# Group norm scales spread by way of memory, and softplus on 128 partitions by 192 columns

## The chip, the cores and the metric

The kernel runs on one core of one Trainium2 chip. The metric is the device time of one execution in microseconds; the figure for the kernel before is the median of three runs. One further execution was profiled, and every row of the trace below comes from it.

## What is computed

The reference is one inference step of a hybrid backbone: two layers over 128 context tokens and 256 latent tokens, with D_MODEL = 1024, all in float32. In each layer a modulated RMS norm is followed by one wide input projection, whose columns feed three mixers (a bidirectional state-space scan, pooling, a spatial gating unit) and three gates; then come an output projection, a residual, and a SwiGLU FFN. Two small pieces of it matter here, both in the scan mixer:

```python
dt = jax.nn.softplus(dt_raw.reshape(bsz, seq, 2, SSD_HEADS) + dt_bias)        # 64 values a token
...
y = y_f + flip(y_b) + xs * d_skip[:, None]
y = y.reshape(bsz, seq, SSD_INNER) * jax.nn.silu(z)
return grouped_rms_norm(y, g_norm, SSD_GROUPS), s_f, s_b                      # 4 groups of 512 channels
```

grouped_rms_norm multiplies each token's 512 channels of a group by 1/sqrt(mean square + eps) and by a gain for each channel.

## The kernel before

All 384 tokens are held at once, as three tiles of 128 (NT = 3, TOK = 384). Activations lie with channels on the partitions and tokens in the columns, so a projection is 8 blocks of 128x128 weights against 384 columns. Each float32 product is made of three float32r matmuls (mm3, L165 to L167): the weights and the activations are split into a rounded high part and a remainder, and high x high, high x low and low x high are summed. The 512 KB weight blocks come in one after another through six raw buffers (L98, on SP's queue); ACT makes the high part (whi, L115), VectorE the remainder (wlo, L116), into four buffers each, three blocks ahead of use (LEAD).

The stage ssd of a layer begins with dt_unit, which projects dt and computes softplus as max(x, 0) + log1p(exp(-|x|)), the logarithm by a polynomial. The weight block of dt holds its 64 columns twice, so the projection fills all 128 partitions of its PSUM tile with two equal halves; before, only the lower 64 are used, with all 384 tokens as columns. From dt follow the running sums (fs), which go out to memory (fsd) and come back spread over the partitions (fb). Then come, group by group (g = 0 to 3), a projection for B and one for C, and four pairs of heads, each with an X and a Z projection; between them stand filler projections whose results are spilled to memory.

The program counts these main units (tick) and posts later steps so many units behind them (post, with the lags L_...). gnorm1 (lag 7) sums the squares of a group over the partitions on TensorE, and VectorE makes the scale of each token from it: yr, 128 tokens by 3, tokens on the partitions. gnorm2 (lag 9) needs these scales along the columns, the same on all partitions. It makes them with three float32 matmuls of yr, broadcast, against the identity (L904), into a PSUM tile of tag tr (two buffers), which ACT copies to the SBUF tile ysq (L906, one buffer, also used for squares). Then VectorE scales the four tiles of the group (ynf, reading yg), and ACT and VectorE split them into yh and yl. sproj (from lag 14) multiplies them with the branch weights. For the last group gnorm1 and gnorm2 stand between fillers, without lags.

TensorE's instructions are issued in the order of the program (manual_schedule); the order on the other engines and on SP's queue, which issues all DMAs of these stages, is set by the planner of the framework from priorities and its own times. Each engine works through its queue in order.

Of the kernel before, what the change touches and what calls it, by code (L numbers as in the profile page):

```python
# [9 lines left out]
F32 = mybir.dt.float32  # L10
# [3 lines left out]
ACTF = mybir.ActivationFunctionType  # L14
ALU = mybir.AluOpType
# [5 lines left out]
NT = 3  # L21
TOK = 384
DEPTH = 2
# [23 lines left out]

FILL = ((3, 0, 2, 2, 1), (2, 1, 1, 2, 1), (1, 0, 1, 2, 1), (0, 0, 1, 1, 0))

L_TURN, L_TURN2, L_CB, L_DEC, L_XN, L_ST, L_Y, L_G1, L_G2, L_SP = 6, 7, 3, 3, 3, 5, 7, 7, 9, 14  # L50
T_G1, T_G2, T_G3 = 1, 1, 2
FIRST = (4,)
M1, M2 = (0, 1), (1, 2)
# [69 lines left out]
class Net:  # L123
# [67 lines left out]
    def build(self):  # L191
        tc, nc, ctx = self.tc, self.nc, self.ctx
        self.base = ctx.enter_context(tc.tile_pool(name="base", bufs=1))
        self.psum = ctx.enter_context(tc.tile_pool(name="psum", bufs=1, space=PSUM))
        self.psbufs = {"mm": 4, "tr": 2, "y": 1, "st": 1}
        dram = ctx.enter_context(tc.tile_pool(name="dram", bufs=1, space=DRAM))
        self.gd = dram.tile([DEPTH, 2, 2, D], F32, name="gd")
        self.xd = dram.tile([DEPTH, NT, 128, D], F32, name="xd")
        self.vd = dram.tile([DEPTH, NT, 128, D], F32, name="vd")
        self.ud = dram.tile([DEPTH, KT, 128, TOK], F32, name="ud")  # L200
        self.thd = dram.tile([DEPTH, 3, KT, 128, TOK], F32, name="thd")
        self.fsd = dram.tile([DEPTH, NH, 2, TOK], F32, name="fsd")
        b = self.base
        self.ident = b.tile([128, 128], F32, name="ident")
        self.mlo = b.tile([128, 128], F32, name="mlo")
        self.mup = b.tile([128, 128], F32, name="mup")
        self.smask = b.tile([64, TOK], F32, name="smask")
        self.edge = b.tile([128, 32], F32, name="edge")
        self.ones = b.tile([128, 1], F32, name="ones")
        self.selm = b.tile([128, 2], F32, name="selm")  # L210
        self.crow = b.tile([128, 2, D], F32, name="crow")

        self.hthl = b.tile([128, 2 * KT * TOK + 32], F32R, name="hthl")
        self.hthi, self.htlo = (self.hthl[:, HO + n * KT * TOK:HO + (n + 1) * KT * TOK].rearrange("p (k t) -> p k t", t=TOK) for n in range(2))
        self.accx = b.tile([128, NT * D], F32, name="accx")
        self.acc = self.accx.rearrange("p (c t) -> p c t", t=TOK)
        self.x = self.accx.rearrange("p (i d) -> p i d", d=D)
        self.flow = Flow(tc, nc, self.io["w"], b)
        self.cp, self.mod, self.xnorm, self.parts, self.vr, self.fnat = {}, {}, {}, {}, {}, {}
        self.pool = None  # L220
        self.flow.add([], self.start)
        for l in range(DEPTH):
            self.layer(l)
        self.flow.run()
        self.close_pool()
# [357 lines left out]
    def ssd(self, l):  # L583
        F = self.flow
        F.add([], lambda: self.ssd_open(l))
        self.main([("dt", l)], lambda w: self.dt_unit(l, w))
        fill = [("u", 0, c) for c in range(KT)] + [("g", br, c) for br in range(3) for c in range(KT)][:3 * KT - ORDER.count("g")]
        def filler(n):
            for _ in range(n):
                if fill:  # L590
                    kind, br, c = fill.pop(0)
                    if kind == "u":
                        self.main([("in", l, C_U + 128 * c)], lambda w, c=c: self.u_spill(l, c, w))
                    else:
                        self.main([("in", l, C_G + D * br + 128 * c)], lambda w, br=br, c=c: self.gate_spill(l, br, c, w))
        for g in range(4):
            self.main([("in", l, C_B + 128 * g)], lambda w, g=g: self.conv_unit(l, 16 + g, w))
            self.main([("in", l, C_C + 128 * g)], lambda w, g=g: self.conv_unit(l, 20 + g, w))
            if g == 0:
                self.post(L_TURN, lambda: self.turn(0))  # L600
                self.post(L_TURN2, lambda: self.turn(1))
            self.post(L_CB, lambda g=g: self.cb_unit(l, g))
            filler(FILL[g][0])
            for t in range(4 * g, 4 * g + 4):
                self.main([("in", l, C_X + 128 * t)], lambda w, t=t: self.conv_unit(l, t, w))
                self.post(L_DEC, lambda t=t: self.decay(l, t))
                self.post(L_XN, lambda t=t: self.xnat(l, t))
                self.post(L_ST, lambda t=t: self.states(l, t))
                self.post(L_Y, lambda t=t: self.ypair(l, t))
                if l == 0 and t < 2:  # L610
                    F.add([], lambda t=t: self.silu_row(t))
                self.take((t % 2 == 1) + (l == 0 and t % 4 == 2))
                self.main([("in", l, C_Z + 128 * t)], lambda w, t=t: self.z_unit(l, t, w))
                if t < 15:
                    filler(FILL[g][1 + t % 4])
            if g == 3:
                break
            self.post(L_G1, lambda g=g: self.gnorm1(l, g))
            self.post(L_G2, lambda g=g: self.gnorm2(l, g))
            for cc in range(4):  # L620
                self.post_main(L_SP + cc, [("brs", l, g, cc)], lambda w, g=g, cc=cc: self.sproj(l, g, cc, w))
        while self.late and len(fill) > T_G1 + T_G2 + T_G3:
            filler(1)
        self.flush_all()
        filler(len(fill) - T_G2 - T_G3)
        F.add([], lambda: self.gnorm1(l, 3))
        filler(len(fill) - T_G3)
        F.add([], lambda: self.gnorm2(l, 3))
        filler(len(fill))
        F.add([], lambda: [self.th_load(l, 0, c) for c in range(3)])  # L630
        for cc in range(4):
            self.main([("brs", l, 3, cc)], lambda w, cc=cc: self.sproj(l, 3, cc, w))
# [53 lines left out]
    def dt_unit(self, l, w):  # L686
# [1 line left out]
        cp = self.cp[l][0]  # L688
        ps = self.ps("mm")
        self.proj(ps, w)  # L690
        zz = self.t(pool, "arg", [128, TOK], 2)[0:64]
        self.act(zz, ps[0:64, 0:TOK], ACTF.Identity, bias=cp[0:64, CP_DTB:CP_DTB + 1])
        e = self.t(pool, "W", [128, 2 * TOK], 2)[0:64, 0:TOK]
        self.act(e, zz, ACTF.Abs)
        self.act(e, e, ACTF.Exp, scale=-1.0)
        mx = self.t(pool, "arg", [128, TOK], 2)[0:64]
        self.ts(mx, zz, 0.0, ALU.max)
        s = self.t(pool, "wb", [128, TOK], 2)[0:64]
        self.ts(s, e, 2.0, ALU.add)
        nc.vector.reciprocal(out=s, in_=s)  # L700
        self.tt(s, s, e, ALU.mult)
        s2 = self.t(pool, "W", [128, 2 * TOK], 2)[0:64, 0:TOK]
        self.tt(s2, s, s, ALU.mult)
        p = self.t(pool, "ysq", [128, TOK], 1)[0:64]
        self.ts(p, s2, 1.0 / 15, ALU.mult)
        for n in (13, 11, 9, 7, 5, 3):
            self.stt(p, p, 1.0 / n, s2, ALU.add, ALU.mult)
        self.stt(p, p, 1.0, s, ALU.add, ALU.mult)
        dtt = self.t(pool, "dtt", [64, TOK], 1)
        self.stt(dtt, p, 2.0, mx, ALU.mult, ALU.add)  # L710
        ea = self.t(pool, "ea", [64, 1], 1)
        self.act(ea, cp[0:64, CP_AL:CP_AL + 1], ACTF.Exp)
        la = self.t(pool, "ysq", [128, TOK], 1)[0:64]
# [177 lines left out]
    def gnorm1(self, l, g):  # L891
        nc, pool = self.nc, self.pool
        sp = self.ps("st")
        for c in range(NT):
            nc.tensor.matmul(sp[:, c:c + 1], lhsT=self.ysum[:, c * 128:(c + 1) * 128], rhs=self.ones, start=True, stop=True)
        ss = self.t(pool, "ss3", [128, NT], 2)
        nc.vector.tensor_copy(out=ss, in_=sp[:, 0:NT])
        self.yr = self.rstd_of(ss, 512, pool)

    def gnorm2(self, l, g):  # L900
        nc, pool = self.nc, self.pool
        rp = self.ps("tr")
        for c in range(NT):
            nc.tensor.matmul(rp[:, c * 128:(c + 1) * 128], lhsT=self.yr[:, c:c + 1].to_broadcast([128, 128]), rhs=self.ident, start=True, stop=True)  # L904
        rb = self.t(pool, "ysq", [128, TOK], 1)
        nc.scalar.copy(out=rb, in_=rp[:, 0:TOK])  # L906
        hls = []
        for t in range(4 * g, 4 * g + 4):
            yn = self.t(pool, "ynf", [128, TOK], 2)
            self.stt(yn, self.yg.pop(t), self.cp[l][0][:, CP_GS + t:CP_GS + t + 1], rb, ALU.mult, ALU.mult)  # L910
            hi = self.t(pool, "yh", [128, TOK], 4, F32R)
            lo = self.t(pool, "yl", [128, TOK], 4, F32R)
            self.split(hi, lo, yn)
            hls.append((hi, lo))
        self.yhl[g] = hls
# [454 lines left out]
```

## Time and profile before

| | before |
|---|---|
| median of 3 runs | 1843.42 us (1841.96 to 1846.58) |
| the profiled execution, time | 1843.37 us |
| the profiled execution, span in the trace | 1841.5 us |
| TensorE, matmul | 1809.9 us busy, 98% of the span, 10724 instructions |
| VectorE | 1448.9 us, 79% |
| ScalarE (ACT) | 969.0 us, 53% |
| weights (raw), from memory | 474 loads of 512 KB |

The profile's page gives busy time by engine, the span in 40 slices, the DMA queues, the chain of work that ended last, the costliest groups of instructions and the DMA issues. The trace behind it can be asked for the waits of an engine, for a timeline of single instructions in a stretch, and for busy times by stretch. A bracket at the end of a row says how long the engine was idle ahead of that instruction and what ended the idle time. Matmuls are pipelined and overlap in the rows, so their cost is read from start to start.

### The profile page before, as it was taken

Reading aid. Unit: us, or ns where it says so; the run is one execution under the profiler, and the core shown is the slowest. Engines: PE = TensorE matmul, PEld = TensorE weight load, DVE = VectorE, ACT = ScalarE, POOL = GpSimd, SP = SyncE. Lnnn points to the kernel's source line nnn. Section 1 sums busy time; section 2 is a strip of 40 time slices with the busy share of each in tenths; the row PEclk is TensorE's granted clock in tenths of the full one; section 3 lists DMA queues with packets and bytes.
Section 4 is the critical chain, followed back from the end, with each engine's and each line's share of the span. In section 5 each row is a group of like instructions: output and inputs, shape, how many; then the busy total and the mean of one; then the engine's idle time right before and its main releaser. Section 6 shows DMA issues by size and latency. Waiting matters only on the chain.

```text
span 1841.5 us, 28979 instructions
## 1 busy us (share of the span) xinstructions
PE 1809.9 (98%) x10724; PEld 1710.4 (93%) x10724; DVE 1448.9 (79%) x2891; ACT 969.0 (53%) x1916; POOL 0.2 (0%) x4
## 2 busy tenths in 40 slices
PE   7999999999999999999999999999999999999998
PEld 4899999999999889889879999999999997998997
DVE  4699989998979687877668989799977797644545
ACT  4687768584443453223355977685834434432332
POOL 0000000000000000000000000000000000000000
PEclk9999999999999999999999999999999999999999
DMA  8666564644757555765545655555455583554441
GB/s 334 236 232 221 187 191 159 212 133 141 265 197 251 171 174 182 247 191 183 191 166 181 223 178 196 158 166 195 133 164 208 189 274 127 170 160 126 126 126 46
DMA packets 112293, 341.15 MB, mean 185 GB/s; under 512 B 12948, under 2 KB 38420, under 8 KB 112024
## 3 DMA queue, kind: packets, MB, share of 16 engines
q1 hardware_dynamic: 112152, 339.30, 56.3%
q8 instruction: 84, 1.38, 0.3%
q14 instruction: 57, 0.47, 0.1%
HBM read 314.38 MB, written 24.87 MB: 184 GB/s over the span
## 4 chain that ended last, share of the span: by engine, by line
PE 91%; DVE 5%; DMA 2%; issue 1%; ACT 1%; SPq 0%; DVEq 0%; ACTq 0%
PE ps_mm L165 22%; PE ps_mm L167 22%; PE ps_mm L166 22%; PE ps_mm L460 5%; PE ps_mm L461 5%; PE ps_mm L462 5%; PE ps_y L879 3%; DMA raw<-w 1%; DVE wlo L116 1%; DVE ajunk L298 1%; PE ps_st L844 1%; PE ps_tr L826 1%; PE ps_mm L1080 1%; PE ps_mm L553 1%; PE ps_mm L555 0%
## 5 line engine op out<-in xcount | busy, mean ns | idle before, releaser
L115 ACT CAST whi<-raw 128x1024 fp32r<-128x1024 f32 x394 | 412.8, 1050 | 535.1 <-PE ps_mm L166 220.7
L165 PE MATMUL ps_mm<-hthl,whi 128*128 128x384 f32 x1936 | 656.6, 339 | 0.0
L167 PE MATMUL ps_mm<-hthl,wlo 128*128 128x384 f32 x1936 | 651.2, 336 | 2.6 <-DVE wlo L116 2.6
L166 PE MATMUL ps_mm<-hthl,whi 128*128 128x384 f32 x1936 | 649.9, 336 | 0.0
L116 DVE TENSOR_TENSOR wlo<-raw,whi 128x1024 fp32r<-128x1024 f32 x394 | 480.9, 1221 | 212.4 <-ACT whi L115 210.9
L167 PEld LDWEIGHTS ps_mm<-hthl,wlo 128*128 128x128 f32 x1936 | 363.8, 188 | 2.9 <-DVE wlo L116 2.9
L165 PEld LDWEIGHTS ps_mm<-hthl,whi 128*128 128x128 f32 x1936 | 364.1, 188 | 2.3 <-issue 1.5
L166 PEld LDWEIGHTS ps_mm<-hthl,whi 128*128 128x128 f32 x1936 | 364.0, 188 | 0.3
L298 DVE CUSTOM_DVE_ANT_0 ajunk<-raw,crow 128x1024 bf16<-128x1024 f32 x160 | 195.4, 1221 | 35.5 <-DMA raw<-w 34.0
L460 PE MATMUL ps_mm<-whi,ah 128*128 128x512 f32 (+1 forms) x360 | 141.4, 393 | 4.8 <-DVE res L147 4.5
L462 PE MATMUL ps_mm<-whi,al 128*128 128x512 f32 (+1 forms) x360 | 141.0, 392 | 0.0
L461 PE MATMUL ps_mm<-wlo,ah 128*128 128x512 f32 (+1 forms) x360 | 140.1, 389 | 0.0
L150 DVE SCALAR_TENSOR_TENSOR ca<-cin,cw,ca 128x388 f32<-128x388 f32 x192 | 118.2, 615 | 2.2 <-ACT ca L144 1.2
L165 PE MATMUL ps_mm<-ah,whi 128*128 128x384 f32 x288 | 98.2, 341 | 0.0
L166 PE MATMUL ps_mm<-al,whi 128*128 128x384 f32 x288 | 96.8, 336 | 0.3 <-DVE al L147 0.3
L167 PE MATMUL ps_mm<-ah,wlo 128*128 128x384 f32 x288 | 96.6, 336 | 0.0
L165 PE MATMUL ps_mm<-yh,whi 128*128 128x384 f32 x256 | 86.9, 339 | 0.0
L460 PEld LDWEIGHTS ps_mm<-whi,ah 128*128 128x128 f32 x360 | 68.3, 190 | 19.4 <-DVE res L147 4.9
L166 PE MATMUL ps_mm<-yl,whi 128*128 128x384 f32 x256 | 86.2, 337 | 0.0
L167 PE MATMUL ps_mm<-yh,wlo 128*128 128x384 f32 x256 | 86.1, 337 | 0.0
L461 PEld LDWEIGHTS ps_mm<-wlo,ah 128*128 128x128 f32 x360 | 68.2, 189 | 14.6
L462 PEld LDWEIGHTS ps_mm<-whi,al 128*128 128x128 f32 x360 | 68.1, 189 | 14.6
(234 smaller groups left out, 2417.1 us busy)
## 6 DMA issues: line engine op xcount, KB each, us to landing
raw<-w SPq DMA_DIRECT2D x474, 512.0 KB, 4.0
fb<-fsd SPq DMA_DIRECT2D x32, 768.0 KB, 4.2
thd<-spill SPq DMA_DIRECT2D x48, 192.0 KB, 4.9
spill<-thd SPq DMA_DIRECT2D x48, 192.0 KB, 4.1
araw<-wa SPq DMA_DIRECT2D x16, 512.0 KB, 8.5
s<-s SPq DMA_DIRECT2D x32, 128.0 KB, 2.1
so<-so SPq DMA_DIRECT2D x32, 128.0 KB, 3.1
k<-gd SPq DMA_DIRECT2D x8, 512.0 KB, 5.1
```

The costliest lines, as they stand in the source:

```text
L115: self.nc.scalar.copy(out=hi, in_=raw)
L116: self.nc.vector.tensor_tensor(out=lo, in0=raw, in1=hi.bitcast(F32), op=ALU.subtract)
L150: self.nc.vector.scalar_tensor_tensor(out=out, in0=a, scalar=s, in1=b, op0=op0, op1=op1)
L165: mm(out, lhsT=whi, rhs=xhi, start=first, stop=False)
L166: mm(out, lhsT=whi, rhs=xlo, start=False, stop=False)
L167: mm(out, lhsT=wlo, rhs=xhi, start=False, stop=last)
L298: self.nc.vector.tensor_tensor_reduce(out=junk, in0=raw, in1=self.crow[:, n, :], scale=0.5, scalar=0.0, op0=ALU.mult, op1=ALU.add, accum_o ...
L460: mm(out, lhsT=xh[:, ts], rhs=hi[:, ws], start=(kk == 0), stop=False)
L461: mm(out, lhsT=xh[:, ts], rhs=lo[:, ws], start=False, stop=False)
L462: mm(out, lhsT=xl[:, ts], rhs=hi[:, ws], start=False, stop=(kk == kn - 1))
L553: mm(av[i, q], lhsT=self.hthi[:, c, t], rhs=hi[:, ws], start=(c == 0), stop=False)
L879: mm(o, lhsT=lt, rhs=rt, start=(n == 0), stop=(n == steps - 1))
```

## The change

The scales of groups 0 to 2 of each layer no longer go over TensorE. gnorm1 ends with a store of yr to a new tensor in memory (grd), laid out so that the 384 tokens of a group stand in a row; a new step gnorm_row (lag 8) loads that row into all 128 partitions of a new tile rb; gnorm2 (now lag 10 instead of 9) uses rb. Group 3 keeps the matmuls, with rb in place of ysq. In dt_unit the lower 64 partitions take tokens 0 to 191 and the upper 64 tokens 192 to 383; softplus runs on 128 by 192, and two ACT copies put the halves side by side again.

```diff
-L_TURN, ..., L_Y, L_G1, L_G2, L_SP = 6, 7, 3, 3, 3, 5, 7, 7, 9, 14
+L_TURN, ..., L_Y, L_G1, L_GR, L_G2, L_SP = 6, 7, 3, 3, 3, 5, 7, 7, 8, 10, 14
...
+        self.grd = dram.tile([DEPTH, 4, NT, 128], F32, name="grd")
...
             self.post(L_G1, lambda g=g: self.gnorm1(l, g))
+            self.post(L_GR, lambda g=g: self.gnorm_row(l, g))
             self.post(L_G2, lambda g=g: self.gnorm2(l, g))
...
-        zz = self.t(pool, "arg", [128, TOK], 2)[0:64]
-        self.act(zz, ps[0:64, 0:TOK], ACTF.Identity, bias=cp[0:64, CP_DTB:CP_DTB + 1])
-        e = self.t(pool, "W", [128, 2 * TOK], 2)[0:64, 0:TOK]
+        HT = TOK // 2
+        zz = self.t(pool, "arg", [128, TOK], 2)[:, 0:HT]
+        for n in range(2):
+            r = slice(64 * n, 64 * n + 64)
+            self.act(zz[r], ps[r, n * HT:(n + 1) * HT], ACTF.Identity, bias=cp[r, CP_DTB:CP_DTB + 1])
+        e = self.t(pool, "W", [128, 2 * TOK], 2)[:, 0:HT]
...
-        mx = self.t(pool, "arg", [128, TOK], 2)[0:64]
+        mx = self.t(pool, "arg", [128, TOK], 2)[:, 0:HT]
...
-        s = self.t(pool, "wb", [128, TOK], 2)[0:64]
+        s = self.t(pool, "wb", [128, TOK], 2)[:, 0:HT]
...
-        s2 = self.t(pool, "W", [128, 2 * TOK], 2)[0:64, 0:TOK]
+        s2 = self.t(pool, "W", [128, 2 * TOK], 2)[:, 0:HT]
...
-        p = self.t(pool, "ysq", [128, TOK], 1)[0:64]
+        p = self.t(pool, "ysq", [128, TOK], 1)[:, 0:HT]
...
+        dth = self.t(pool, "wb", [128, TOK], 2)[:, 0:HT]
+        self.stt(dth, p, 2.0, mx, ALU.mult, ALU.add)
         dtt = self.t(pool, "dtt", [64, TOK], 1)
-        self.stt(dtt, p, 2.0, mx, ALU.mult, ALU.add)
+        for n in range(2):
+            nc.scalar.copy(out=dtt[:, n * HT:(n + 1) * HT], in_=dth[64 * n:64 * n + 64])
...
         self.yr = self.rstd_of(ss, 512, pool)
+        if g < 3:
+            nc.sync.dma_start(out=self.grd[l, g].rearrange("c p -> p c"), in_=self.yr)
+
+    def gnorm_row(self, l, g):
+
+        self.rb = self.t(self.pool, "rb", [128, TOK], 1)
+        self.nc.sync.dma_start(out=self.rb, in_=self.grd[l, g].rearrange("c p -> (c p)").partition_broadcast(128))
 
     def gnorm2(self, l, g):
         nc, pool = self.nc, self.pool
-        rp = self.ps("tr")
-        for c in range(NT):
-            nc.tensor.matmul(rp[:, c * 128:(c + 1) * 128], lhsT=self.yr[:, c:c + 1].to_broadcast([128, 128]), rhs=self.ident, start=True, stop=True)
-        rb = self.t(pool, "ysq", [128, TOK], 1)
-        nc.scalar.copy(out=rb, in_=rp[:, 0:TOK])
+        if g < 3:
+            rb = self.rb
+        else:
+            rp = self.ps("tr")
+            for c in range(NT):
+                nc.tensor.matmul(rp[:, c * 128:(c + 1) * 128], lhsT=self.yr[:, c:c + 1].to_broadcast([128, 128]), rhs=self.ident, start=True, stop=True)
+            rb = self.t(pool, "rb", [128, TOK], 1)
+            nc.scalar.copy(out=rb, in_=rp[:, 0:TOK])
```

## Rows read from the trace of the kernel before

**Rows 1.** The page, busy time by engine: us (share) x instructions.

```profile
span 1841.5 us, 28979 instructions
PE 1809.9 (98%) x10724; PEld 1710.4 (93%) x10724; DVE 1448.9 (79%) x2891; ACT 969.0 (53%) x1916; POOL 0.2 (0%) x4
```

**Rows 2.** The waits of TensorE: us in total, times, longest.

```profile
PE ps_mm L460 <- DVE res L147: 4.5, 1, 4.5
PE ps_mm L167 <- DVE wlo L116: 2.6, 1, 2.6
...
PE ps_tr L328 <- ACT ysq L906: 0.7, 1, 0.7
...
PE ps_tr L783 <- DVE ct L150: 0.2, 1, 0.2
```

**Rows 3.** Busy time by stretch, group 2 of layer 1: stretch, length, each engine.

```profile
1295.00:1330.00 35.00, 35.00 (x248) 33.97 (x247) 34.09 (x88) 31.75 (x83) 0.00 (x0) 1.00 0.44 139
```

**Rows 4.** Timeline of TensorE at gnorm2, group 0, layer 0: start, us, instruction.

```profile
199.98 0.33 PE L167 MATMUL ps_mm<-hthl,wlo 128*128 128x384 f32 x1
200.15 0.83 PE L904 MATMUL ps_tr<-ident,s3y 128*128 128x128 f32 x6
200.74 0.42 PE L165 MATMUL ps_mm<-hthl,whi 128*128 128x384 f32 x1
```

**Rows 5.** DMA issues: KB each, median us from issue to landing.

```profile
fb<-fsd SPq DMA_DIRECT2D x32, 768.0 KB, 4.2
thd<-spill SPq DMA_DIRECT2D x48, 192.0 KB, 4.9
...
fsd<-fs SPq DMA_DIRECT2D x4, 48.0 KB, 1.5
```

**Rows 6.** Timeline of SP's queue, group 2 of layer 1.

```profile
1304.27 0.33 SPq L798 DMA_DIRECT2D fb<-fsd  x1
1310.03 0.33 SPq L98 DMA_DIRECT2D raw<-w  x1
```

**Rows 7.** Timeline of VectorE, group 2 of layer 1.

```profile
1303.02 0.15 DVE L150 SCALAR_TENSOR_TENSOR s3y<-s3t,s3y 128x3 f32<-128x3 f32 x1
...
1307.68 1.15 DVE L150 SCALAR_TENSOR_TENSOR ynf<-yg,cp,ysq 128x384 f32<-128x384 f32 x2
...
1323.80 1.22 DVE L116 TENSOR_TENSOR wlo<-raw,whi 128x1024 fp32r<-128x1024 f32 x1
```

**Rows 8.** Timeline of TensorE, third matmul of the first sproj of that group.

```profile
1328.57 0.34 PE L167 MATMUL ps_mm<-yh,wlo 128*128 128x384 f32 x1
```

**Rows 9.** Timeline of VectorE, start of ssd in layer 1.

```profile
977.66 1.22 DVE L116 TENSOR_TENSOR wlo<-raw,whi 128x1024 fp32r<-128x1024 f32 x1 [1.14 <-ACT whi L115]
...
983.40 2.54 DVE L700 RECIPROCAL wb<-wb 64x384 f32<-64x384 f32 x1
...
990.59 0.27 DVE L150 SCALAR_TENSOR_TENSOR bt<-th,ca 128x128 f32<-128x128 f32 x1
990.79 0.54 DVE L150 SCALAR_TENSOR_TENSOR ysq<-ysq,W 64x384 f32<-64x384 f32 x1
991.26 0.41 DVE L150 SCALAR_TENSOR_TENSOR bt<-th,ca 128x256 f32<-128x256 f32 x1
991.59 0.54 DVE L150 SCALAR_TENSOR_TENSOR ysq<-ysq,W 64x384 f32<-64x384 f32 x1
...
995.07 1.21 DVE L116 TENSOR_TENSOR wlo<-raw,whi 128x1024 fp32r<-128x1024 f32 x1
...
999.57 1.20 DVE L116 TENSOR_TENSOR wlo<-raw,whi 128x1024 fp32r<-128x1024 f32 x1
```

**Rows 10.** Timeline of TensorE, same stretch: the waiting matmul, and that of the next block.

```profile
996.33 0.44 PE L167 MATMUL ps_mm<-hthl,wlo 128*128 128x384 f32 x1 [2.63 <-DVE wlo L116]
...
1001.59 0.34 PE L167 MATMUL ps_mm<-hthl,wlo 128*128 128x384 f32 x1
```

**Rows 11.** Timeline of ACT, same stretch.

```profile
1001.00 0.99 ACT L144 ACTIVATE wt<-fs,fe 64x128 f32<-64x128 f32 x3 [5.39 <-DVE fe L723]
```

More of the change, by code (lines that the diff above doesn't have):

```diff
@@ L48 @@
 FILL = ((3, 0, 2, 2, 1), (2, 1, 1, 2, 1), (1, 0, 1, 2, 1), (0, 0, 1, 1, 0))
-L_TURN, L_TURN2, L_CB, L_DEC, L_XN, L_ST, L_Y, L_G1, L_G2, L_SP = 6, 7, 3, 3, 3, 5, 7, 7, 9, 14
+L_TURN, L_TURN2, L_CB, L_DEC, L_XN, L_ST, L_Y, L_G1, L_GR, L_G2, L_SP = 6, 7, 3, 3, 3, 5, 7, 7, 8, 10, 14
 T_G1, T_G2, T_G3 = 1, 1, 2
```

## The prediction

> **What bounds the kernel now.** I read the page's table of engines first: TensorE is busy 1809.9 of the 1841.5 us span [rows 1]. It is the engine to follow, and its instructions are issued in the order of the program. So I then listed all that TensorE waited for [rows 2]. Behind the first 17 us, in which the inputs come in, the waits that bear on this case are few: 4.5 us for a residual product (L460 on res), 2.6 us for a weight split (L167 on wlo), 0.7 us for a PSUM slot (L328 on ysq), 0.2 us for the first B/C product (L783 on ct). Two more, for the norm ahead of the FFN, are untouched; all the rest is matmul after matmul. Two things can therefore shorten the run: an instruction taken out of TensorE's stream, or one of these waits. Work that is saved on another engine counts only through a wait. The third view, busy time by stretch, shows a second limit close by: around the group norm of group 2 in layer 1 VectorE is busy 34.09 of 35.00 us [rows 3]. What makes VectorE stand still there is not easily caught up.
>
> **Part 1, what leaves TensorE.** gnorm2 makes three float32 matmuls (L904), six records, that spread yr over the partitions. In the timeline L904 starts at 200.15, where the next L165 would have started (the matmul before began at 199.98, and they follow 0.17 apart), and L165 starts at 200.74 [rows 4]. That is 0.59 us of TensorE's time. Groups 0 to 2 of two layers lose them: 6 x 0.59 = 3.5 us. Group 3 keeps them. Nothing on TensorE takes their place.
>
> The copy L906 from PSUM goes with them, six times. It hides behind other ACT work nearly everywhere; the one place where TensorE waited for it is L328, 0.7 us, in group 1 of layer 0, where the transposition in ada_end wanted the PSUM slot that L906 was still reading [rows 2]. With one tr tile fewer the slot it gets was read long before. I count 0.7 us.
>
> **Part 2, what the row costs by way of memory.** Added are six stores of yr (384 separate numbers) and six broadcast loads of 192 KB, all on SP's queue; SP must hold the load until the store has landed. The trace has no store in such small pieces. Bounds: the smallest store with a landing time is fs to fsd, 1.5 us; the slowest small one is the spill, 4.9 us. The load is like fb from fsd, also a broadcast from memory, 4.2 us [rows 5]. With some 0.3 us for each issue [rows 6] the row is there 0.3 + 1.5 + 0.3 + 4.2 = 6.3 us to 0.3 + 4.9 + 0.3 + 4.2 = 9.7 us after yr, if SP is free. I take 6.3 to 7, since the store is nearest to that of fs (few bytes, from VectorE's result).
>
> The Trainium skill (DMA: Bandwidth & Descriptors, Rules for kernel authors) says that a transfer whose last dimension is not contiguous is cut into one descriptor per element, and should be rearranged; no run here shows such a store. By the same page's 10.5 ns a packet (Bandwidth) 384 pieces would take an estimated 4.0 us, inside the bounds above, and the sum stays.
>
> Who needs the row: only the four ynf products on VectorE, and behind them sproj. Before, in group 2 of layer 1, yr was done at 1303.2 and the first ynf began at 1307.7 [rows 7], 4.5 us later. gnorm2 is now posted one unit later (10 for 9); a unit is 24 matmuls of 0.17 us, 4.1 us at least. So ynf's turn comes some 8.6 us after yr, and the row is there in 6.3 to 9.7: hidden, or late by a us. And sproj, which uses what ynf makes, reaches its third matmul only at 1328.57, 20 us after the first ynf [rows 7, 8]. So I cost the detour at nothing (a gain is excluded: nobody gets the row sooner than before); its cover is the unit by which gnorm2 is put off. If the cover is gone, VectorE stands still and the weight splits behind ynf in its queue are late; that is priced as a rival. What SP queues behind the waiting load are raw weights, state loads and spills.
>
> rb also gets a buffer of its own and leaves ysq to the squares; TensorE waits for no square, so it counts nothing. The tiles that move up in the pool (ynf, yh, yl) are used again only late in the next stage.
>
> **Part 3, softplus.** Its 14 operations on VectorE up to dt halve in columns (192 for 384); the reciprocal is one of them. They stand at the start of ssd, once a layer. In layer 1 TensorE waits there 2.63 us, at 996.33, for the split wlo that VectorE began at 995.07, 17 us after the split before (977.66), just behind the chain's operations, with which those of the first two convolutions alternate without idle time [rows 9, 10]. So VectorE's time before 995.07 is on the path.
>
> What a narrower operation saves I take from starts, since VectorE overlaps ends: a 64x384 operation holds it 0.47 us (990.79 to 991.26), a 128x128 one 0.20 (990.59 to 990.79), a 128x256 one 0.33 (991.26 to 991.59) [rows 9]. So time goes by columns, and 192 columns come to about 0.265, a saving of 0.205. Between the reciprocal and 995.07 there are nine such (two products, seven fused ones): 1.85 us. The reciprocal takes 2.54 us for 384 columns [rows 9]; the trace has no other width, so its saving lies between 0 and 1.27; I take 1.27, as 6.6 ns a column is far above what an instruction's start can cost. The three tensor_scalars I leave at nothing. Sum 3.1 us: the split ends at 993.2 instead of 996.3, and TensorE wanted it at 996.33 - 2.63 = 993.70 [rows 9, 10]. The whole 2.6 us go, with half a us to spare; without the reciprocal's share 0.7 us of it would stay.
>
> What is late next is the split after it: it starts at 999.57, ends near 1000.8, and its matmul (1001.59) comes 2.6 us earlier, at 998.96 [rows 9, 10]. It gains the same 3.1 us plus 0.2 for the last product (dth), and loses what the detour of dt over ACT adds. That detour is two copies of 64x192; three 64x128 ones take 0.99 us [rows 11], so about 0.7 us. 1000.8 - 3.3 + 0.7 = 998.2, still in time. On ACT itself there are three operations more and two narrower ones, about 0.7 us a layer; ACT already waits 5.39 us in this very place for the chain's end [rows 11], so they hide in that. The copies' wait for dth queues spills and roundings behind it on ACT, for less than those 5.39 us. In layer 0 the same chain costs TensorE only the 0.2 us at L783 [rows 2], which goes too.
>
> **The sum.** 3.5 + 0.7 + 2.6 + 0.2 = 7.0 us. The profiled execution took 1843.37 us, of which 1841.5 is the span; its time stands at the median of the runs (1843.42), so no correction: 1843.4 - 7.0 = 1836.4 us. The wait at L460 [rows 2] and the two for the norm lie in the back part, which the change doesn't touch; they stay.
>
> **Rivals.** (a) Only the matmuls and L328 count; the wait of layer 1 stays or moves. The order on VectorE, ACT and SP is planned anew when operations change length, and a split may just be put behind other work; the margin is half a us. For it: in layer 1 a weight split stood 17 us behind the one before (977.66, then 995.07 [rows 9]), so the planner does let it slip. Against it: the sum of the work before it falls. 1843.4 - 4.2 = 1839.2 us.
>
> (b) The row comes late and VectorE stands still: the one that ends on the other side. Place: group 2, where the split that ends at 1324.9 is wanted at 1328.57, a margin of 3.6 us [rows 7, 8]; I take the same for layer 0, whose code is the same. Before, SP stood from 1304.6 to 1310.03 waiting for a raw buffer [rows 6]. If the store falls behind that, it is issued at 1310.4, lands 1.5 to 4.9 us later, and the row is there at 1316.4 to 1319.8, against ynf's turn at about 1311.8: VectorE stands 4.6 to 8 us. Beyond the margin TensorE loses 1 to 4.4 us, in both layers 2 to 8.8: 1838.4 to 1845.2 us, and 1845.2 is the rival's time. It passes the time before when the stand exceeds 7.1 us in both layers. The Trainium skill (DMA: Bandwidth & Descriptors, Rules for kernel authors) speaks for it: a DMA that reads what another wrote has to wait on the issuing engine for the first one's completion, so all that SP has behind it waits too; the trace of before has no such pair next to each other. Against it: the row is asked for two units ahead, so the planner has room to put the store first.
>
> (c) The change brings more: with other orders the 4.5 us of L460 [rows 2] go as well: 1836.4 - 4.5 = 1831.9 us. Nothing in the change is near it.
>
> (d) The change does not do what it says, for instance the planner puts ynf no later than before, so that the row is on the path from the start. Then all six groups wait a little, but only group 2 pays; this falls in (b).
>
> **How the numbers follow.** Chances: forecast 0.46, (a) 0.26, (b) 0.20, (c) 0.08. Predicted is the forecast, 1836.4. The range 1833.0 to 1843.5 leaves out (c) and the worst third of (b), about 0.15, and holds the ends for the reciprocal and the store. A measurement of this kernel tells some 0.3%, 5.5 us, from no change, so faster means under 1837.9. The forecast lies only 1.5 us below that: of its 0.46 I give 0.37 to faster and 0.09 to the same, of (a) 0.04 to faster, of (b) 0.01, all of (c): faster 0.50. Slower by over 5.5 us needs (b) at its worst and another wait: 0.06. The same: 0.44.
>
> **What would show it.** Right: six L904 groups gone and L165 following at 0.17; no wait at L328; the wait of L167 on wlo under half a us; 64x384 operations replaced by 128x192 ones that hold VectorE near 0.27 us and a reciprocal near 1.3; ynf begins without idle time of VectorE. Wrong: VectorE idle before ynf with a DMA of rb as its releaser, or SP held long between store and load; new waits of TensorE on wlo near 421 or 1328; a reciprocal much above 1.3 us; a wait that comes up in the back part.

## The result, and the profile after

The changed kernel takes 1876.01 us (1870.90 to 1879.35) against 1843.52 us of the kernel before in the same measurement: a ratio of 1.0171, interval 1.0157 to 1.0184. It is 32 us slower where 1836.4 us were forecast. The profiled execution took 1874.14 us; its span is 30.9 us longer than the 1841.5 us before [rows 1].

The page, busy time by engine:

```profile
span 1872.4 us, 28934 instructions
PE 1817.2 (97%) x10688; PEld 1713.5 (92%) x10688; DVE 1439.8 (77%) x2891; ACT 963.2 (51%) x1916; POOL 0.2 (0%) x4
```

TensorE has 36 records fewer (10688 for 10724: the six groups of six), VectorE and ACT are less busy, and yet the span grows. So look at waits, not at work. The waits of TensorE after (us in total, times, longest), to be held against [rows 2]:

```profile
PE ps_y L888 <- DVE se L147: 8.6, 4, 5.0
PE ps_y L888 <- DVE yg L150: 8.5, 3, 4.6
...
PE ps_tr L835 <- ACT bn L788: 2.3, 2, 2.0
PE ps_st L853 <- DVE ss L906: 2.2, 2, 1.3
PE ps_mm L167 <- DVE wlo L116: 2.1, 2, 1.4
...
PE ps_st L853 <- DVE xw L147: 1.8, 1, 1.8
```

None of these six stands in the list before, apart from wlo, whose wait there was another one (below). They lie in the groups, and come to 25.5 us. Two thirds are on ps_y, the product of a pair of heads (ypair, L888), which needs VectorE's se, or a PSUM slot that VectorE's yg must first have read. What VectorE and SP wait for there, first VectorE's list and then SP's:

```profile
DVE ynf L150 <- DMA rb<-grd: 47.4, 6, 8.9
```

```profile
SPq L914 <- DMA grd<-s3y: 49.4, 6, 9.5
```

VectorE stands before ynf in all six groups, 7.9 us each time on average, for the loaded row; and SP stands before the load, 8.2 us each, for the store to land. TensorE's stands of 3 us and more on ps_y lie in groups 0 and 2 of both layers; in groups 1 VectorE stands as long (5.94 and 8.19 us), but TensorE waits for it not at all in layer 0 and 1.6 us in layer 1. Group 0 of layer 0, in the timelines of SP, VectorE and TensorE:

```profile
199.93 0.38 SPq L909 DMA_DIRECT2D grd<-s3y  x1
201.06 0.34 SPq L98 DMA_DIRECT2D raw<-w  x1
209.44 0.33 SPq L914 DMA_DIRECT2D rb<-grd  x1
```

```profile
206.02 0.55 DVE L150 SCALAR_TENSOR_TENSOR sz<-th,ps_mm 128x384 f32<-128x384 f32 x1
215.42 1.15 DVE L150 SCALAR_TENSOR_TENSOR ynf<-yg,cp,rb 128x384 f32<-128x384 f32 x2 [8.85 <-DMA rb<-grd]
...
218.95 0.42 DVE L147 TENSOR_TENSOR se<-se,ps_st 128x256 f32<-128x256 f32 x1
```

```profile
214.01 0.39 PE L888 MATMUL ps_y<-cf,s 128*64 128x128 f32 x4
219.42 0.48 PE L888 MATMUL ps_y<-cf,se 128*64 128x128 f32 x2 [5.03 <-DVE se L147]
```

From store to load SP takes 9.5 us (209.44 - 199.93), from load to row 6 us. Over the six groups the first is 9.5, 9.5, 10.5, 10.0, 9.9 and 9.1 us. VectorE reaches ynf at 206.6 and stands 8.85 us. The pair of heads is due in the meantime; its se is only a 0.42 us sum, but it is queued behind ynf. TensorE stands 5.03 us.

Then a second loss begins. Busy time by stretch (stretch, length, engines, granted clock, DMA share, GB/s):

```profile
214.00:216.00 2.00, 0.39 (x8) 0.15 (x4) 0.58 (x2) 0.00 (x0) 0.00 (x0) 1.00 0.13 46
216.00:218.00 2.00, 0.00 (x0) 0.00 (x0) 2.00 (x6) 1.93 (x5) 0.00 (x0) 0.55 0.08 30
218.00:220.00 2.00, 0.58 (x6) 0.58 (x8) 2.00 (x5) 2.00 (x6) 0.00 (x0) 0.50 0.38 136
220.00:222.00 2.00, 2.00 (x16) 1.67 (x13) 2.00 (x8) 2.00 (x8) 0.00 (x0) 0.50 0.00 0
222.00:224.00 2.00, 2.00 (x11) 2.00 (x10) 2.00 (x4) 2.00 (x5) 0.00 (x0) 0.74 0.95 316
```

While TensorE stands, its granted clock falls to 0.50, the lower of its two levels (1.2 of 2.4 GHz), and stays there for some 3 us after the work goes on: in 220 to 222 it is fully busy at half speed. In the groups there are five such stretches (the first from 216.22, the last up to 1359.68). Taken together:

```profile
sum 23.85, PE 19.76 PEld 17.87 DVE 23.85 ACT 21.95 POOL 0.00; mean PE 3.95 PEld 3.57 DVE 4.77 ACT 4.39 POOL 0.00
```

Of the 23.85 us TensorE is busy for 19.76, so the lower clock costs it at most half of that, 9.9 us; in the other 4 us it stands anyway, and these are in the waits already. In the kernel before there is no such stretch in the groups.

The account: 25.5 us of waits, less the 0.7 at L328 that are gone, plus 9.9 of clock, less 4.0 of matmuls (six times 0.66, as measured below) and 2.8 of softplus waits, is 27.9; the spans differ by 30.9. The 3 us that are left are not worked out here.

### The profile page after: what moved, and what is told of

It is laid out like the page before. It is cut to its first block, busy times and chain, and to the rows that moved or that the text cites. A ratio compares the mean times of both kernels' runs of the same rounds, so it can differ in the third digit from the quotient of the medians.

```text
span 1872.4 us, 28934 instructions
## 1 busy us (share of the span) xinstructions
PE 1817.2 (97%) x10688; PEld 1713.5 (92%) x10688; DVE 1439.8 (77%) x2891; ACT 963.2 (51%) x1916; POOL 0.2 (0%) x4
## 4 chain that ended last, share of the span: by engine, by line
PE 80%; DVE 9%; DMA 7%; issue 2%; ACT 1%; SPq 0%; DVEq 0%; ACTq 0%
PE ps_mm L165 19%; PE ps_mm L166 19%; PE ps_mm L167 19%; PE ps_mm L462 5%; PE ps_mm L461 5%; PE ps_mm L463 5%; DMA grd<-s3y 3%; PE ps_y L888 2%; DVE wlo L116 2%; DMA raw<-w 2%; DMA rb<-grd 1%; DMA s<-s 1%; DVE ajunk L299 1%; DVE ca L150 1%; DVE wb L150 1%
## 5 line engine op out<-in xcount | busy, mean ns | idle before, releaser
L159 ACT CAST ah<-t 128x384 fp32r<-128x384 f32 x72 | 36.8, 512 | 92.7 <-DVE t L150 60.6
```

Of the source, the lines that this page charges most:

```text
L159: self.nc.scalar.copy(out=hi, in_=x)
```

## The experiments

Theory after the result: the 384 single numbers of the store land slowly; VectorE, which takes its queue in order, stands behind ynf for the row, and the operations behind it are what TensorE needs. Rivals: part of the loss is the softplus part's; SP, held between store and load, is the cause; any round trip through memory takes that long. Ratios are against the kernel before, run beside each kernel.

**Softplus alone** (the edits of gnorm1, gnorm_row and gnorm2 undone).

> Only the softplus part of the change; the scales go over TensorE as in the kernel before. Theory (the loss lies wholly in the row by way of memory, the softplus part brings what the trace of after shows): layer 1's wait of 2.6 us and the 0.2 us at L783 go, so about 1843.5 - 2.8 = 1840.7 us, ratio 0.9985. Rival (the two ACT copies and the wider partitions cost elsewhere, part of the 31 us is theirs): 1843.5 or above.

Measured: 1841.41 us, ratio 0.9983 (0.9974 to 0.9992), some 3 us faster than the 1844.26 beside it. TensorE's wait on wlo and the one at L783 are gone. This part does what the forecast said.

**The row alone** (the edits of dt_unit undone).

> Only the row by way of memory; softplus stays on 64 by 384. Theory: all of the loss is here: 1876.0 + 2.8 = about 1879 us (ratio 1.019), again with SP held 9 to 10.5 us between store and load and VectorE idle 8 to 9 us ahead of ynf. Rival (the two parts disturb each other, the order planned for one makes the other late): clearly below 1876.

Measured: 1881.27 us, ratio 1.0212 (1.0194 to 1.0229); VectorE's idle time before ynf is 51.8 us. All of the loss is here, 37 us where 36 were expected.

**The row loaded, but not read:**

```diff
-L_TURN, ..., L_GR, L_G2, L_SP = 6, 7, 3, 3, 3, 5, 7, 7, 8, 10, 14
+L_TURN, ..., L_GR, L_G2, L_SP = 6, 7, 3, 3, 3, 5, 7, 7, 8, 9, 14
...
-        if g < 3:
-            rb = self.rb
-        else:
-            rp = self.ps("tr")
...
+        rp = self.ps("tr")
...
+        rb = self.t(pool, "ysq", [128, TOK], 1)
+        nc.scalar.copy(out=rb, in_=rp[:, 0:TOK])
```

> As after, with the store and the load of the row in place, but nothing reads the loaded row: gnorm2 makes its scales with the matmuls of the kernel before, at the old lag. It separates the queue from the consumer. Theory (VectorE stands behind ynf for the row, and ypair and TensorE behind VectorE): without the reader the loss goes, about 1840 to 1843 us, although SP is still held 9 to 10 us between store and load. Rival (SP held is what costs: raw weights, state loads and spills behind the load come late): 1865 to 1876 us stays.

Measured: 1852.27 us, ratio 1.0043 (1.0028 to 1.0059). Between the two: without the reader some two thirds of the loss go, but 11 us against softplus alone stay. In the traces of the two kernels TensorE runs level (within 0.02 us) through both groups 0 and both groups 1; it loses 1.4 us in group 2 of layer 0 and 7.5 in group 2 of layer 1 (the other 2 us lie in the FFN). Group 2 of layer 1 on SP, on ACT and on TensorE:

```profile
1308.67 0.38 SPq L909 DMA_DIRECT2D grd<-s3y  x1
1309.73 0.32 SPq L807 DMA_DIRECT2D fb<-fsd  x1
1318.31 0.32 SPq L914 DMA_DIRECT2D rb<-grd  x1
...
1319.67 2.15 SPq L805 DMA_DIRECT2D s<-s  x1
```

```profile
1327.44 0.83 ACT L144 ACTIVATE se<-s,et 128x64 f32<-128x64 f32 x3 [7.52 <-DMA s<-s]
```

```profile
1333.98 0.77 PE L853 MATMUL ps_st<-xw,bn 128*128 128x256 f32 x1 [2.66 <-DVE xw L147]
```

The state load (L805) stands behind the held load of the row, is issued at 1319.67, and ACT waits 7.52 us for it; VectorE's chain of the next pair waits for ACT, and TensorE 2.66 us for xw, after which its clock is down again. So the store and the load cost something of their own, by what stands beside and behind them, but less, and mostly where VectorE has no slack: this is the group that was full before [rows 3]. Whether that is the hold of SP's queue this run doesn't tell: the state load, once issued, is itself used only 7.8 us later.

**The row from GpSimd's queue** (store and load issued there; SP is free).

> As after, but the store and the load of the row are issued from GpSimd's queue, which has nothing else to do; SP is never held by them. It takes the queue's share out of the 32 us. Theory (the reader on VectorE carries most; the held queue adds state loads and raw loads that come late, 8 to 11 us as where the row was loaded and not read): the row is as late as in after, VectorE idle 7 to 10 us before ynf, 1862 to 1870 us. Rival (the queue is the cause, VectorE's stand a side effect): 1845 us or below.

Measured: 1881.92 us, ratio 1.021 (1.0183 to 1.0236): no better, rather worse than after, and outside both expectations: the 8 to 11 us of the held queue did not come back. That SP is held is not the main cause. The DMA issues of this kernel (KB, median us to landing), and VectorE's list:

```profile
rb<-grd POOLq DMA_DIRECT2D x6, 192.0 KB, 5.5
grd<-s3y POOLq DMA_DIRECT2D x6, 1.5 KB, 9.8
```

```profile
DVE ynf L150 <- DMA rb<-grd: 56.7, 6, 10.8
```

The 1.5 KB store lands after 9.8 us from this queue too, and the row is still later. What is beside it is slowed as well. Stretches of this kernel behind the last store (issued at 1331.26; the load follows at 1341.63):

```profile
1334.00:1336.00 2.00, 2.00 (x24) 1.75 (x25) 2.00 (x6) 2.00 (x8) 0.00 (x0) 1.00 1.06 25
1336.00:1338.00 2.00, 2.00 (x23) 1.78 (x20) 0.58 (x1) 2.00 (x6) 0.00 (x0) 1.00 1.20 28
1338.00:1340.00 2.00, 2.00 (x13) 2.00 (x12) 0.00 (x0) 0.09 (x1) 0.00 (x0) 1.00 0.72 22
```

The last two columns are DMA share and GB/s. SP is not held here, and a load of 768 KB (fb) was issued at 1331.94, yet the DMA engines move 22 to 28 GB/s.

**Fewer, longer pieces.** Two kernels. In the first, each partition writes its three numbers as one piece of 12 bytes; in the second, yr is transposed first:

```diff
-            nc.sync.dma_start(out=self.grd[l, g].rearrange("c p -> p c"), in_=self.yr)
+            nc.sync.dma_start(out=self.grd[l, g].rearrange("c p -> (c p)").rearrange("(p c) -> p c", c=NT), in_=self.yr)
```

```diff
-            nc.sync.dma_start(out=self.grd[l, g].rearrange("c p -> p c"), in_=self.yr)
...
     def gnorm_row(self, l, g):
...
+        tp = self.ps("tr")
+        self.nc.tensor.transpose(out=tp[0:NT, 0:128], in_=self.yr, identity=self.ident)
+        row = self.t(self.pool, "rb", [128, TOK], 1)[0:NT, 0:128]
+        self.nc.scalar.copy(out=row, in_=tp[0:NT, 0:128])
+        self.nc.sync.dma_start(out=self.grd[l, g], in_=row)
```

> As after, but the store writes yr as it lies, 128 pieces of 12 bytes in place of 384 of 4 bytes; the row then holds the scales of a group in another order of tokens, so the output is another. It separates the number of pieces from the round trip as such. Theory (the landing goes by pieces): of the 9 to 10.5 us between store and load on SP some 5 us go (about 4 to 5 us remain), VectorE's idle time before ynf falls from 8-9 to 3-4 us, time about 1846 to 1855. Rival (any store followed by a load of what it wrote holds SP that long): 9 us stay, 1876 us.

> As after, but yr (128 by 3) is first transposed on TensorE to 3 by 128, copied by ACT, and stored in 3 pieces of 512 bytes; load and reader as in after. Theory (the hold on SP goes by the number of pieces: 9.0 to 10.5 us with 384, 4.0 to 6.4 with 128): 2 to 3.5 us between store and load, VectorE's idle time before ynf 0 to 2 us; but the transposition stands on TensorE one unit after gnorm1 and may wait 0 to 1.5 us for yr, six times: 1838 to 1849 us. Rival (a fixed round trip to memory of 4 us or more, whatever the pieces): SP held 4 us or more, 1846 us or above.

Measured: 1845.88 us (1.001; 1.000 to 1.0019) and 1860.35 us (1.0092; 1.0071 to 1.0114). SP's waits for the store, of the kernel with 12 bytes and of the one that transposes, and then TensorE's waits of the latter:

```profile
SPq L914 <- DMA grd<-s3y: 22.3, 6, 5.4
```

```profile
SPq L919 <- DMA grd<-rb: 6.8, 5, 2.9
```

```profile
PE ps_tr L914 <- DVE s3y L150: 11.0, 4, 3.4
PE ps_tr L914 <- ACT arg L144: 4.6, 1, 4.6
PE ps_tr L914 <- ACT cin L756: 1.4, 1, 1.4
```

From store to load, mean of the six groups: 9.75 us with 384 pieces (9.1 to 10.5), 5.2 with 128 (4.0 to 6.4), 2.8 with 3 (1.4 to 3.6). That is 18 ns a piece between the first two ((9.75 - 5.2) / 256) and 19 between the last two: the landing goes by the number of pieces, on top of some 2.8 us. With 128 pieces about 30 of the 32 us are gone by that alone. The transposition's own plan failed at another place: at lag 8 TensorE asks for yr before VectorE has it, 17.0 us in all (where the rows name ACT, VectorE's last s3y also ends only 0.15 us ahead of the transposition). VectorE's idle time before ynf is nil there, so the row was in time.

**More cover, the same pieces** (gnorm2 at lag 12).

> As after, but gnorm2 is posted at lag 12 in place of 10: two units of 4.1 us or more, 8.2 us more cover for the row, with the same pieces and the same queue. Theory (what was missing is 6 to 9 us of cover in each group, and the held queue costs apart from that): VectorE's idle time before ynf 0 to 1 us, the stands of ypair gone in five of the six groups, the late state load of group 2 stays, 1843 to 1851 us. Rival (cover does not help, since the pieces slow all transfers or ynf just moves onto the weight splits of sproj): 1860 us or above.

Measured: 1858.27 us, ratio 1.0069 (1.0046 to 1.0093), more than expected, and the step on the idle time was wrong: VectorE still stands up to 7.3 us before ynf. In groups 0 and 1, where it stands, TensorE waits not at all (0) or 0.7 us (1) all the same. The row comes nearly as late after its store as in after (13.5 to 14.7 us, for 13.7 to 15.6), but less stands between it and se (VectorE, group 0 of layer 1):

```profile
1124.89 0.62 DVE L150 SCALAR_TENSOR_TENSOR ynf<-yg,cp,rb 128x384 f32<-128x384 f32 x1 [7.08 <-DMA rb<-grd]
...
1126.42 0.41 DVE L147 TENSOR_TENSOR se<-se,ps_st 128x256 f32<-128x256 f32 x1
```

se starts 1.5 us behind the first ynf, against 3.5 us in the rows of after above, and TensorE's ps_y begins at 1127.02 without a wait. The loss lies in group 2, where ynf doesn't wait. Group 2 of layer 1, SP, ACT and TensorE:

```profile
1314.65 0.38 SPq L909 DMA_DIRECT2D grd<-s3y  x1
1315.71 0.32 SPq L807 DMA_DIRECT2D fb<-fsd  x1
1323.59 0.32 SPq L914 DMA_DIRECT2D rb<-grd  x1
```

```profile
1327.78 0.40 ACT L144 ACTIVATE arg<-fb,nf 128x128 f32<-128x128 f32 x1 [4.68 <-DMA fb<-fsd]
```

```profile
1333.87 0.48 PE L888 MATMUL ps_y<-W,xn 128*64 128x128 f32 x2 [3.67 <-DVE yg L150]
```

fb was issued before SP was held, 1.1 us behind the store, and is used 12.1 us later; such loads landed in 3.8 to 5.0 us before ([rows 5] has the median), and in 5.6 to 6.7 with softplus alone, as far as the traces know their landings. The stretches of this kernel show why:

```profile
1316.00:1318.00 2.00, 2.00 (x14) 2.00 (x13) 2.00 (x8) 1.99 (x5) 0.00 (x0) 1.00 2.62 49
1318.00:1320.00 2.00, 2.00 (x29) 1.76 (x29) 2.00 (x6) 2.00 (x8) 0.00 (x0) 1.00 0.00 0
1320.00:1322.00 2.00, 2.00 (x20) 1.78 (x17) 2.00 (x5) 1.87 (x5) 0.00 (x0) 1.00 1.07 43
```

The DMA engines are occupied (a packet counts with all its time where it starts, hence 2.62 and 0.00), but move 0 to 49 GB/s with 768 KB waiting. The small pieces don't only land late themselves, they hold up what is beside them. The held queue can't be the reason: fb went out ahead of it, and with the row on GpSimd's queue, where SP is free, the stretches above are as slow. It goes with the pieces: the longest landing of an fb load that the traces know is 11.1 to 12.6 us in the four kernels with 384 pieces from SP's queue, 8.0 to 8.2 in the four with 128, and 5.0 to 7.4 in the three with 3 or none. What the held queue costs beside that, no experiment tells.

**12 bytes with cover.** VectorE reads the row of the 12-byte store with a stride of three, so that the tokens are in order again; gnorm2 at lag 12, then at lag 11, then at lag 12 for groups 0 and 1 alone, group 2 keeping its matmuls at lag 9:

```diff
-            nc.sync.dma_start(out=self.grd[l, g].rearrange("c p -> p c"), in_=self.yr)
+            nc.sync.dma_start(out=self.grd[l, g].rearrange("c p -> (c p)").rearrange("(p c) -> p c", c=NT), in_=self.yr)
...
+                self.stt(yn.rearrange("i (c p) -> i c p", c=NT), self.yg.pop(t).rearrange("i (c p) -> i c p", c=NT), self.cp[l][0][:, CP_GS + t:CP_GS + t + 1], rb.rearrange("i (p c) -> i c p", c=NT), ALU.mult, ALU.mult)
```

> Nothing left out: the store writes yr as it lies, 128 pieces of 12 bytes, the load is the same, and VectorE reads the loaded row with a stride of three numbers; gnorm2 at lag 12. Theory (both costs go with fewer pieces and more cover): SP held 4 to 6.4 us, no idle time before ynf, 1836 to 1841 us. Rival (the strided read doubles the 0.61 us of ynf, 24 of them on VectorE, and VectorE is full in group 2; or any hold on SP costs there): 1843 us or above.

> As the kernel with the 12-byte store, the strided read and lag 12, but gnorm2 at lag 11. It asks whether two units of extra cover were too many: at lag 12 the split yl of group 2 was ready 1.1 us late for sproj, in both layers. Theory (the row is there within 4 to 6.4 us of hold plus a load of some 4, so one unit of extra cover just does): no wait of TensorE on yl, VectorE idle 0 to 1.5 us before ynf, 1837 to 1841 us. Rival (at lag 11 the row is late again in groups where SP is held longest, VectorE stands there): 1842 us or above.

> 12-byte store, strided read and lag 12 for groups 0 and 1; group 2, where VectorE is full, keeps the three matmuls at lag 9 as in the kernel before. Theory (in groups 0 and 1 the matmuls and the L328 wait are pure gain, 4 x 0.6 + 0.7 = 3.1 us, and group 2 is where any detour is paid): 1841.0 - 3.1 = about 1838 us, ratio to before 0.9970. Rival (the hold on SP costs wherever it is, or planning shifts the loss elsewhere): 1841 us or above.

Measured, in this order: 1840.83 us, 0.9985 (0.9974 to 0.9996); 1844.53 us, 0.9998 (0.9985 to 1.0010); 1839.18 us, 0.9967 (0.9954 to 0.9979). In the trace of the first, against that of softplus alone, TensorE gains 0.66 us in each of groups 0 and 1, and in group 1 of layer 0 another 0.85 (L328); in group 2 it loses 0.6 and 2.9 us. Lag 11 is no cure and misses the 1837 to 1841 us expected: its loss moves to xw (4.4 us of waits) as the row is late again (13.8 us of idle time before ynf). Without the row in group 2 the gain of the others stays. The strided read is not free: a ynf that reads the row so takes 0.75 us on average for 0.61.

**The transposition one unit later** (lag 9, gnorm2 at lag 11).

> As the kernel that transposes yr on TensorE and stores 3 pieces of 512 bytes, but the transposition one unit later (lag 9) and gnorm2 at lag 11. There TensorE waited 17 us in all for yr at lag 8. Theory (those 17 us were TensorE asking too early; at lag 9, where the matmuls of the kernel before stood without a wait, they go): waits at the transposition under 1 us in all, 1838 to 1843 us. Rival (the copy and the row are then late for ynf): VectorE idle before ynf 2 us or more in some groups, 1846 us or above.

Measured: 1837.90 us, ratio 0.9967 (0.9954 to 0.9980), just below what was expected, with all six groups by way of memory. TensorE's wait at the transposition, and VectorE's before ynf:

```profile
PE ps_tr L914 <- DVE s3y L150: 0.2, 1, 0.2
```

```profile
DVE ynf L150 <- DMA rb<-grd: 4.1, 4, 2.6
```

VectorE's longest stand, 2.6 us, is what the rival asked for, but TensorE loses nothing by it: it gains 0.56 us in five of the six groups, and 0.84 more at L328. The last two kernels beat both the kernel before and the changed one; between them the runs show no difference.

## Why the prediction was wrong

**Bound and views: right.** TensorE's stream and its few waits set the time, and group 2 of layer 1 had no slack.

**Part 1: right, a little low.** The six groups of matmuls are gone and L328's wait too. The traces show 0.66 us a group for 0.59, and 0.85 for 0.7.

**Part 2: the step that failed, twice.** First the price: the landing of the store was bounded by 1.5 us (fs to fsd) and 4.9 us (the spill) and taken near 1.5, "since the store is nearest to that of fs (few bytes, from VectorE's result)". It measured 9 to 10.5 us from issue to issue. Bytes were the wrong likeness: what costs is the 384 pieces, and neither row had such pieces. The row came 15.5 us after the store (215.42 - 199.93), not 6.3 to 9.7. The text had the warning: the Trainium skill (DMA: Bandwidth & Descriptors, Rules for kernel authors) says that a transfer with a last dimension that isn't contiguous becomes one descriptor an element. The page of the profile agrees; its count of packets, of softplus alone, of the 12-byte store, and of after:

```profile
DMA packets 112293, 341.15 MB, mean 185 GB/s; under 512 B 12948, under 2 KB 38420, under 8 KB 112024
```

```profile
DMA packets 114022, 342.35 MB, mean 186 GB/s; under 512 B 13908, under 2 KB 40148, under 8 KB 113752
```

```profile
DMA packets 115558, 342.35 MB, mean 183 GB/s; under 512 B 15444, under 2 KB 41684, under 8 KB 115288
```

After has 1536 small packets more than the 12-byte kernel, 256 a group: 384 - 128. But the estimate of 4.0 us by the same page's 10.5 ns a packet (Bandwidth), a figure of a load of 64 packets issued from GpSimd, was less than half of what was measured, about 18 ns a piece and 2.8 us beside; the measurement decides.

Second the cover: "Who needs the row: only the four ynf products on VectorE, and behind them sproj". That lists the readers of the row; of what stands behind the waiting instruction in its queue, the text names only the weight splits. se, yg and W of the next pair of heads stand there too, and TensorE wants them within a few us, not 20.

A third term was named but stood at nothing: what the store and the load do to other transfers ("What SP queues behind the waiting load are raw weights, state loads and spills"). With the row loaded and not read, 11 us stayed against softplus alone.

**Part 3: right.** The 128x192 operations and the reciprocal of after, VectorE, start of ssd in layer 1 (for [rows 9]):

```profile
994.95 1.35 DVE L706 RECIPROCAL wb<-wb 128x192 f32<-128x192 f32 x1
...
997.29 0.34 DVE L147 TENSOR_TENSOR wb<-wb,W 128x192 f32<-128x192 f32 x1
997.55 0.62 DVE L150 SCALAR_TENSOR_TENSOR ca<-cin,cw,ca 128x388 f32<-128x388 f32 x1
```

0.26 us from start to start, where 0.265 was worked out; the reciprocal saves 1.19 us, where 1.27 was taken. The 2.6 us wait of layer 1 [rows 10] is gone; two small ones (nf 0.5, dtc 0.4 us) are new.

**The sum.** Its gains were there: the two kernels in which the row is cheap (one of them with four of the six rows) stand at 0.9967, 1837.3 us by the kernel before of the prediction, for 1836.4.

**The rivals.** (b) had the mechanism, VectorE standing before ynf, and the sign. It was too small by its own terms: a landing of at most 4.9 us, a stand counted in group 2 alone and against the weight split wlo, at 1328.57, with a margin of 3.6 us. The stand of 7.9 us came in all six groups and was paid on ypair, in groups 0 and 2 of both layers, and a stand of TensorE could bring the fall of its clock, up to 9.9 us that no rival had. So 1845.2 as its worst, and 0.06 for slower, were far off. (a) and (c) did not occur; (d) needs no place: the row was late by its landing, not by its posting.

## What to carry to other kernels

Price a small DMA by its pieces, not by its bytes: count the contiguous runs, and make the row contiguous (transpose, or let the reader take the stride) before it goes to memory. When an instruction of an in-order engine may wait, list what stands behind it in the queue and when the bounding engine wants that; the readers of its result are the smaller question. And add to a stand of TensorE what its lower clock costs after it.

## What the runs showed of the hardware

Stores in 4-byte pieces took about 18 ns a piece and slowed their neighbours: beside one, a 768 KB load was used 12.1 us after its issue (such loads landed in 3.8 to 5.0 us before, in 5.6 to 6.7 with softplus alone), while the DMA engines moved 0 to 49 GB/s. Issued from GpSimd's queue they did the same, 22 to 28 GB/s.

A stand of TensorE can cost more than its length: beside 25.5 us of waits, up to 9.9 us went at the lower granted clock. Not each stand is followed by it: the one of 5.03 us was, the 2.0 us on bn and the 2.63 us on wlo of the kernel before [rows 10] were not. The Trainium skill (TensorE: Matmul & The Clock Gate, Part 1) says that the clock is gated by how busy the engine has been; the rows agree, as every fall in the groups of after comes in a stand of TensorE or within half a us behind one, and the kernel before, which stands there for 0.7 us at most, keeps 1.00.
